# Moving side products of a three-branch recurrent layer by a chunk, and two score products into one PSUM tile

## The chip, the cores and the metric

The kernel runs on one core of a Trainium2 chip. The time is device time in microseconds (us), from start to end of one execution. TensorE (PE) multiplies matrices into PSUM, VectorE (DVE), ScalarE (ACT) and GpSimd (POOL) do the rest, and SyncE (SP) issues most of the loads and stores.

## The reference

Two groups of tokens, a prompt of 256 and 8 sequences of 8 sample tokens, go through two layers of width 2048. One combined input projection feeds three branches, each gated by a SiLU path; three merge gates weigh their projections:

```python
xn = _rmsnorm(x, lp['norm_g'])
proj = (xn @ lp['w_in']).astype(jnp.float32)
u_s5, z_s5, u_lru, z_lru, q, k, v, z_ret, g_s5, g_lru, g_ret = jnp.split(proj, splits, axis=-1)
y_s5, ns_re, ns_im = _s5(u_s5, ...)
y_lru, n_lru, n_conv = _rglru(u_lru, ...)
y_ret, n_ret = _retention(q, k, v, r_ret, pos0, lp['ret_gn_g'])
b_s5 = (y_s5 * jax.nn.silu(z_s5)) @ lp['w_branch_s5']
b_lru = (y_lru * jax.nn.silu(z_lru)) @ lp['w_branch_lru']
b_ret = (y_ret * jax.nn.silu(z_ret)) @ lp['w_branch_ret']
merged = sigmoid(g_s5) * b_s5 + sigmoid(g_lru) * b_lru + sigmoid(g_ret) * b_ret
out = merged @ lp['w_out']
return (x + out), ns_re, ns_im, n_lru, n_conv, n_ret
```

The parts that the change touches are, in `_rglru`, the two block-diagonal gates of the convolved input `xc`

```python
xb = xc.reshape(bsz, s, LRU_BLOCKS, LRU_BLOCK)
r = jax.nn.sigmoid(jnp.einsum('bsnc,ncd->bsnd', xb, w_a).reshape(bsz, s, LRU_WIDTH) + b_a)
i = jax.nn.sigmoid(jnp.einsum('bsnc,ncd->bsnd', xb, w_x).reshape(bsz, s, LRU_WIDTH) + b_x)
```

and in `_retention` (8 heads of 128) the scores and the new state

```python
sc = jnp.einsum('bihd,bjhd->bhij', qc, kc) * dmask[None]
inner = jnp.einsum('bhij,bjhe->bihe', sc, vc)
r_new = r * g_chunk + jnp.einsum('bjhd,bjhe->bhde', kc * zeta[None, :, :, None], vc)
```

## The kernel before

The prompt and sample tokens stand together as 320 columns. The large products run as one main stream on TensorE: the weights come in blocks of 256 output columns, in chunks of 512 input rows (`raw`, 512 KB each, loaded by SP). Each half chunk is split into a high part (`whi`, made by ScalarE, L125) and a low part (`wlo`, made by VectorE, L98) and multiplied three ways into a main PSUM tile `pt`: L1423 (high by high), L1424 (high weight by low input) and L1425 (low weight by high input), 12 matmuls of 320 columns a half chunk, 24 a chunk. Inputs are `xh` and `xl`, or `yhl` for the branch projections of the merge.

Everything else is side work. It is written as Python generators that are advanced once after each half chunk (`step`); a plain `yield` waits two such steps, so a piece behind it is emitted one chunk, 24 main matmuls, later. The order on every engine and queue is the order of emission, fixed when the program is built. Side products take a PSUM tile `ps` of [128, 512] from a pool of four (`ps()`); a fifth must wait until the readers of the first are done.

- `lru_u` convolves the LRU's input on VectorE into `xc` (tile `lxc`), then multiplies it by the gates' weights at L804, one pair of blocks `j` at a time.
- `ret_heads` takes a pair of heads `m`: the prompt's scores of each head go into a tile of their own (L970, L971, columns 0 to 383), the sample scores of both heads into a third (L974), from `kd`, a copy of the sample columns of `k` (tile `rkd`). VectorE reads the sample scores into `scs` and the prompt's scores into `rsc`. Then `k` is transposed (L994) for the state.
- `ret_state` takes the sample states `r0` (in rows, `r`) and adds two products per head (L1108); the result is stored as `ret_s`. Just before, transposes of the pair's output (L1076) go to `z`.
- `merge_blocks` orders the blocks of a merge: gate blocks lead the branch projections by `n` blocks.

The `ret_state` of one pair and the `ret_heads` of the next meet on the engines: four pairs a layer, three such handovers.

Of the kernel before, what the change touches and what calls it, by code (L numbers as in the profile page):

```python
# [20 lines left out]
SEQ, NB, NS, PAST = 256, 8, 8, 2048  # L21
# [57 lines left out]
class Program:  # L79
# [687 lines left out]
    def lru_u(self, l, j, pt):  # L767
        nc, I = self.nc, self.I
        u = self.wt([128, 2, PADW], name="lu")
        self.mul(u[:, :, 3:S0], pt[:, :, :SEQ], self.rs2()[:, :, :SEQ])  # L770
        us = u[:, :, S0:].rearrange("p n (b e) -> p n b e", e=11)
        for n in range(2):
            self.mul(us[:, n, :, 3:], pt[:, n, SEQ:T].rearrange("p (b s) -> p b s", s=NS),
                     self.rstd[:, SEQ:].rearrange("p (b s) -> p b s", s=NS))
        nc.vector.memset(u[:, :, 0:3], 0.0)
        while not self.flag.get(('lru', l)):
            yield
        for n in range(2):
            self.copy(us[:, n, :, 0:3], self.lin[:, 2 * j + n, 0:24].rearrange("p (b k) -> p b k", k=3))
        yield  # L780
        wg = self.wt([128, 2, 2, 128], name="lw")
        nc.sync.dma_start(wg, I['lw'][l, j])
        xc, r, i = [], [], []
        while j and not self.flag.get(('y', l, 0, j - 1)):
            yield
        for n in range(2):
            b = 2 * j + n
            x = self.vt([128, CONVW], name="lxc")
            self.ts(x, u[:, n, 0:CONVW], self.pcol(l, 'convw', b), OP.mult, self.pcol(l, 'convb', b), OP.add)
            for k in range(1, 4):  # L790
                yield 0
                self.stt(x, u[:, n, k:k + CONVW], self.pcol(l, 'convw', 8 * k + b), x, OP.mult, OP.add)
            xc.append(x)
            self.copy(self.lst[:, b, 9:12], u[:, n, SEQ:SEQ + 3])
            self.copy(self.lst[:, b, 12:36].rearrange("p (b k) -> p b k", k=3), us[:, n, :, 8:11])
            yield
        for n in range(2):
            b = 2 * j + n
            r.append(self.vt([128, CONVW + 8], name="lr"))
            i.append(self.vt([128, CONVW], name="li"))  # L800
            pp = []
            for k, dst, key in ((0, r[n][:, :CONVW], 'ba'), (1, i[n], 'bx')):
                p = self.ps()
                nc.tensor.matmul(p[:, :CONVW], wg[:, k, n], xc[n], start=True, stop=True)  # L804
                pp.append((dst, p, key))
            yield
            for dst, p, key in pp:
                self.act(dst, p[:, :CONVW], AF.Sigmoid, bias=self.pcol(l, key, b))
        yield
        while not self.flag.get(('sp', l)):  # L810
            yield
        for n in range(2):
            self.mul(i[n], i[n], xc[n])
            yield 0
        for n in range(2):
            self.act(xc[n], r[n][:, :CONVW], AF.Exp, scale=self.sp8[:, 2 * j + n:2 * j + n + 1])
        yield
        for n in range(2):
            t = r[n][:, :CONVW]
            self.act(t, t, AF.Tanh, scale=self.sp4[:, 2 * j + n:2 * j + n + 1])  # L820
        yield
        for n in range(2):
            self.stt(xc[n], xc[n], 1.0, r[n][:, :CONVW], OP.add, OP.mult)
            yield n
        for n in range(2):
            t = r[n][:, :CONVW]
            self.act(t, t, AF.Sqrt)
            self.ts(xc[n], xc[n], -1.0, OP.mult, 1.0, OP.add)
        yield
        for n in range(2):  # L830
            t = r[n][:, :CONVW]
            self.stt(t, xc[n], 1.0, t, OP.add, OP.mult)
            yield 0
            self.mul(i[n], i[n], t)
            nc.vector.memset(xc[n][:, S0 - 1:S0 + 77:11], 0.0)
            nc.vector.tensor_copy(i[n][:, S0 - 1:S0 + 77:11], self.lin[:, 2 * j + n, 24:32])
            yield 0
            self.dve(xc[n], 2.1)
            nc.vector.tensor_tensor_scan(r[n][:, :CONVW], xc[n], i[n], 0.0, op0=OP.mult, op1=OP.add)
            yield 0  # L840
        while not self.flag.get(('zl', l, j)):
            yield
        z = self.szl.pop(j)
        for n in range(2):
            h = r[n]
            self.copy(self.lst[:, 2 * j + n, 0:1], h[:, SEQ - 1:SEQ])
            self.copy(self.lst[:, 2 * j + n, 1:9], h[:, S0 + 7:S0 + 85:11])
            self.mul(z[:, n, :SEQ], z[:, n, :SEQ], h[:, :SEQ])
            zs = z[:, n, SEQ:].rearrange("p (b s) -> p b s", s=NS)
            self.mul(zs, zs, h[:, S0:S0 + 88].rearrange("p (b e) -> p b e", e=11)[:, :, 0:NS])  # L850
            yield 0
        self.y_parts(l, 0, j, z)
        self.nl += 1
        if self.nl == 4:
            yield
            nc.sync.dma_start(self.O['lru'][l], self.lst)
# [96 lines left out]
    def ret_heads(self, l, m):  # L953
        nc, I, O, sm = self.nc, self.I, self.O, self.sm
# [8 lines left out]
        q, k = self.ret.pop(('q', m)), self.ret.pop(('k', m))  # L963
        kd = self.vt([128, 2, 64], name="rkd")
        self.copy(kd, k[:, :, SEQ:])
        k4 = self.parts_of(k)
        pp, sc = [], []
        for n in range(2):
            p = self.ps()
            nc.tensor.matmul(p[:, :256], k[:, n, 0:128], q[:, n, 0:256], start=True, stop=True)  # L970
            nc.tensor.matmul(p[:, 256:384], k[:, n, 128:256], q[:, n, 128:256], start=True, stop=True)  # L971
            pp.append(p)
        p = self.ps()
        nc.tensor.matmul(p[:, :128], kd.rearrange("p n t -> p (n t)"), q[:, :, SEQ:], start=True, stop=True)  # L974
        yield
        scs = self.scs
        for n in range(2):
# [4 lines left out]
        for n in range(2):  # L982
            t = self.vt([128, 384], name="rsc")
# [6 lines left out]
        for n in range(2):  # L990
            h = 2 * m + n
            p = self.ps()
# [6 lines left out]
        p = self.rows_of(k4)  # L999
# [21 lines left out]
        for n in range(2):  # L1021
            p = self.ps()
# [8 lines left out]
                             start=True, stop=False, skip_group_check=True)  # L1031
            po.append(o)
        for n in range(2):
            o = po[n]
            for h in range(2):
                for g in range(4):
                    nc.tensor.matmul(o[g * 32:(g + 1) * 32, 2], self.qpad[:, n, 2 * g + h], r0[n][:, 2 * g + h],  # L1037
                                     start=False, stop=h == 1, tile_position=(0, g * 32), skip_group_check=True)
# [12 lines left out]
        v, rs, t = (vv[:, i] for i in range(3))  # L1051
# [20 lines left out]
        for n in range(2):  # L1072
            h = 2 * m + n
            p = self.ps()
# [11 lines left out]
    def ret_state(self, l, m, kt, k4, vt, v4, r0):  # L1086


        nc, O, sm = self.nc, self.O, self.sm
        p = self.ps()  # L1090
        for n in range(2):
            for c in range(2):
                nc.tensor.matmul(p[:, n * 128:(n + 1) * 128], kt[:, n, c], vt[:, n, c], start=c == 0, stop=c == 1,  # L1093
                                 skip_group_check=True)
        yield
        rp = self.vt([128, 2, 128], name="rp")
        self.copy(rp.rearrange("p n e -> p (n e)"), p[:, :256])
        yield
        nc.sync.dma_start(O['ret_p'][l][:, 2 * m:2 * m + 2], rp)
        for n in range(2):  # L1100
            h = 2 * m + n
            for b in range(4):
                r = slice(32 * b, 32 * b + 32)
                self.copy(self.vbd[r, :, b], v4[r, n].bitcast(F32))
            yield
            for c in range(2):
                p = self.ps()
                nc.tensor.matmul(p, k4[:, n, c * 128:(c + 1) * 128], self.vbd[:, c].rearrange("p b e -> p (b e)"),  # L1108
                                 start=True, stop=True)
                yield  # L1110
                rr = r0[n][:, 4 * c:4 * c + 4].rearrange("p b e -> p (b e)")
                self.stt(rr, rr, self.g8[h], p, OP.mult, OP.add)
            nc.sync.dma_start(O['ret_s'][l, h], r0[n])
        self.flag['st', l, m] = True
# [145 lines left out]
    def merge_blocks(self, l, br, inp, wb, yb, cg):  # L1260
        def br_blk(j):
            return (wb[j], 8, yb, self.merge, (l, br, j))
        n = 3 if l == 0 and br == 0 else 1
        for j in range(8 + n):
            if j < 8:
                yield inp(cg + 256 * j, self.gate, j)
            if j >= n:
                yield br_blk(j - n)
# [276 lines left out]
```

## Time and profile before

| | us |
|---|---|
| median of 3 runs (2424.43 to 2430.43) | 2425.45 |
| the profiled execution's own time | 2425.49 |
| its span | 2423.7 |
| PE busy | 2369.4 (98%) |
| DVE busy | 1533.1 (63%) |
| ACT busy | 1107.3 (46%) |
| POOL busy | 588.4 (24%) |

The span is the part of the execution that the trace covers. A busy share is a mean over the whole span; what ends a wait is read at each place. [...]

### The profile page before, as it was taken

Reading aid. Unit: us, or ns where it says so; the run is one execution under the profiler, and the core shown is the slowest. Engines: PE = TensorE matmul, PEld = TensorE weight load, DVE = VectorE, ACT = ScalarE, POOL = GpSimd, SP = SyncE. Lnnn points to the kernel's source line nnn. Section 1 sums busy time; section 2 is a strip of 40 time slices with the busy share of each in tenths; the row PEclk is TensorE's granted clock in tenths of the full one; section 3 lists DMA queues with packets and bytes.
Section 4 is the critical chain, followed back from the end, with each engine's and each line's share of the span. In section 5 each row is a group of like instructions: output and inputs, shape, how many; then the busy total and the mean of one; then the engine's idle time right before and its main releaser. Section 6 shows DMA issues by size and latency. Waiting matters only on the chain. (4 is left out here: it accounts for less than half of the span.)

```text
span 2423.7 us, 44413 instructions
## 1 busy us (share of the span) xinstructions
PE 2369.4 (98%) x16778; PEld 2340.4 (97%) x16778; DVE 1533.1 (63%) x2830; ACT 1107.3 (46%) x2019; POOL 588.4 (24%) x1159
## 2 busy tenths in 40 slices
PE   9999999989999999999999999999999999999997
PEld 9999899989999999999999999999999999999997
DVE  7885658656664756755557765866665656555544
ACT  6655444434443534444455564444434434444443
POOL 2020007999211000300100000699930200000011
PEclk9999999999999999999999999999999999999999
DMA  6754775455445545445545587454454554444453
GB/s 229 222 155 144 195 217 168 141 171 171 149 157 174 188 152 172 148 157 196 193 158 187 171 218 209 146 174 151 139 191 162 174 181 160 149 149 150 155 175 130
DMA packets 154023, 413.72 MB, mean 171 GB/s; under 512 B 18640, under 2 KB 60112, under 8 KB 153552
## 3 DMA queue, kind: packets, MB, share of 16 engines
q1 hardware_dynamic: 153232, 410.16, 53.0%
q8 instruction: 132, 2.16, 0.4%
q10 hardware_dynamic: 576, 0.72, 0.1%
q14 instruction: 83, 0.68, 0.1%
HBM read 373.83 MB, written 31.74 MB: 167 GB/s over the span
## 5 line engine op out<-in xcount | busy, mean ns | idle before, releaser
L98 DVE TENSOR_TENSOR wlo<-raw,whi 128x512 fp32r<-128x512 f32 (+1 forms) x1199 | 854.3, 721 | 800.7 <-ACT whi L125 789.8
L125 ACT ACTIVATE whi<-raw 128x512 fp32r<-128x512 f32 (+1 forms) x1199 | 745.8, 629 | 1070.0 <-PE pt L1424 923.0
L1423 PE MATMUL pt<-xh,whi 128*128 128x320 f32 x3352 | 1053.9, 314 | 1.4 <-ACT whi L125 0.9
L1424 PE MATMUL pt<-xl,whi 128*128 128x320 f32 x3352 | 1042.2, 311 | 0.8 <-DVE xl L118 0.8
L1425 PE MATMUL pt<-xh,wlo 128*128 128x320 f32 x3352 | 1042.3, 311 | 0.2 <-DVE wlo L98 0.2
L1423 PEld LDWEIGHTS pt<-xh,whi 128*128 128x128 f32 x3352 | 635.6, 190 | 7.0 <-issue 4.1
L1424 PEld LDWEIGHTS pt<-xl,whi 128*128 128x128 f32 x3352 | 635.4, 190 | 4.8 <-DVE xl L118 1.5
L1425 PEld LDWEIGHTS pt<-xh,wlo 128*128 128x128 f32 x3352 | 634.8, 189 | 0.9 <-DVE wlo L98 0.7
L1423 PE MATMUL pt<-yhl,whi 128*128 128x320 f32 x768 | 239.3, 312 | 2.7 <-ACT yhl L125 2.7
L1425 PE MATMUL pt<-yhl,wlo 128*128 128x320 f32 x768 | 238.0, 310 | 2.9 <-DVE wlo L98 2.9
L1424 PE MATMUL pt<-yhl,whi 128*128 128x320 f32 x768 | 238.1, 310 | 0.2 <-DVE yhl L98 0.2
L598 POOL TENSOR_TENSOR cs<-H,l2r 128x64 f32<-128x64 f32 x254 | 122.5, 482 | 253.2 <-DVE H L112 233.5
L271 POOL TENSOR_TENSOR acc<-acc,sq 128x320 f32<-128x320 f32 x28 | 25.6, 914 | 591.7 <-ACT sq L125 590.6
L1423 PE MATMUL pt<-M,whi 128*128 128x320 f32 x512 | 158.4, 309 | 0.0
L1425 PE MATMUL pt<-M,wlo 128*128 128x320 f32 x512 | 158.2, 309 | 0.0
L1424 PE MATMUL pt<-M,whi 128*128 128x320 f32 x512 | 158.2, 309 | 0.0
L1423 PEld LDWEIGHTS pt<-yhl,whi 128*128 128x128 f32 x768 | 144.8, 188 | 3.6 <-ACT yhl L125 2.9
L1425 PEld LDWEIGHTS pt<-yhl,wlo 128*128 128x128 f32 x768 | 144.7, 188 | 3.1 <-DVE wlo L98 3.1
L1424 PEld LDWEIGHTS pt<-yhl,whi 128*128 128x128 f32 x768 | 144.8, 188 | 0.6 <-DVE yhl L98 0.6
L601 POOL TENSOR_TENSOR H<-cs,cs 128x64 f32<-128x64 f32 x254 | 121.1, 477 | 19.9
L599 POOL TENSOR_TENSOR cs<-H,l2i 128x64 f32<-128x64 f32 x254 | 119.9, 472 | 0.0
L600 POOL TENSOR_TENSOR cs<-cs,H 128x64 f32<-128x64 f32 x254 | 118.1, 465 | 0.0
(255 smaller groups left out, 2445.2 us busy)
## 6 DMA issues: line engine op xcount, KB each, us to landing
raw<-w_in SPq DMA_DIRECT2D x447, 512.0 KB, 4.2
raw<-w_out SPq DMA_DIRECT2D x64, 512.0 KB, 4.1
raw<-wb_lru SPq DMA_DIRECT2D x32, 512.0 KB, 4.1
raw<-wb_ret SPq DMA_DIRECT2D x32, 512.0 KB, 3.8
raw<-wb_s SPq DMA_DIRECT2D x32, 512.0 KB, 3.6
r<-sret SPq DMA_DIRECT2D x16, 512.0 KB, 5.2
ret_s<-r SPq DMA_DIRECT2D x16, 512.0 KB, 3.0
raw<-w_glu SPq DMA_DIRECT2D x16, 512.0 KB, 3.6
```

The source lines that it names most:

```text
L98: self.nc.vector.tensor_tensor(o, a, b, op=op)
L125: self.nc.scalar.activation(o, a, f, **k)
L271: self.nc.gpsimd.tensor_tensor(self.acc, self.acc, sq, op=OP.add)
L598: g.tensor_tensor(t1, old, lr, op=OP.mult)
L599: g.tensor_tensor(t2, self.swap(old), li, op=OP.mult)
L600: g.tensor_tensor(t1, t1, new, op=OP.add)
L601: g.tensor_tensor(new, t1, t2, op=OP.add)
L1423: nc.tensor.matmul(o, hi[:, kk, cs], xh, start=k == 0, stop=False)
L1424: nc.tensor.matmul(o, hi[:, kk, cs], xl, start=False, stop=False)
L1425: nc.tensor.matmul(o, lo[:, kk, cs], xh, start=False, stop=k == nk - 1)
```

## The change

Five edits. The gate products of `lru_u` stand one more `yield` behind the last write of `xc`. In `ret_heads` a `yield` stands between the copy `kd` and the scores, and the sample scores go into columns 384 to 511 of the first head's tile rather than into a tile of their own. In `ret_state` a second `yield` stands ahead of the products of each head. In the first merge of layer 0 four gate blocks lead, where three did.

```diff
@@ -794,6 +794,7 @@
             self.copy(self.lst[:, b, 12:36].rearrange("p (b k) -> p b k", k=3), us[:, n, :, 8:11])
             yield
+        yield
         for n in range(2):
             b = 2 * j + n
@@ -963,6 +964,7 @@
         kd = self.vt([128, 2, 64], name="rkd")
         self.copy(kd, k[:, :, SEQ:])
+        yield
         k4 = self.parts_of(k)
@@ -970,8 +972,8 @@
             pp.append(p)
-        p = self.ps()
-        nc.tensor.matmul(p[:, :128], kd.rearrange("p n t -> p (n t)"), q[:, :, SEQ:], start=True, stop=True)
+        p = pp[0][:, 384:]
+        nc.tensor.matmul(p, kd.rearrange("p n t -> p (n t)"), q[:, :, SEQ:], start=True, stop=True)
         yield
@@ -1102,6 +1104,7 @@
                 self.copy(self.vbd[r, :, b], v4[r, n].bitcast(F32))
             yield
+            yield
             for c in range(2):
@@ -1260,7 +1263,7 @@
-        n = 3 if l == 0 and br == 0 else 1
+        n = 4 if l == 0 and br == 0 else 1
```

Line numbers of the changed kernel are one to three higher: L804 becomes L805, L970 and L971 become L972 and L973, L974 becomes L976, L994 becomes L996, L1076 becomes L1078, L1108 becomes L1111 and L1423 becomes L1426.

TensorE at the first handover of layer 0, before. `ps_6535` takes transposes that `z` will read, `ps_6544` and `ps_6547` the next pair's scores, `ps_6550` the sample scores, `ps_6571` the last state product; the rows left out are main matmuls.

```order
L1076 MATMUL ps_6535<-ident_603,ron_6333 128x128 x3
L970 MATMUL ps_6544<-ra_6199,ra_6378 128x256 [waits DVE_49]
L971 MATMUL ps_6544<-ra_6199,ra_6378 128x128
L970 MATMUL ps_6547<-ra_6199,ra_6378 128x256 [waits PE_49]
L971 MATMUL ps_6547<-ra_6199,ra_6378 128x128
L974 MATMUL ps_6550<-ra_6199,rkd_6539 128x128 [waits DVE_49,Activation_49]
L1423 MATMUL pt_6518<-xh_164,whi_6479 128x320
...
L1108 MATMUL ps_6571<-vbd_5306,rk4_5975 128x512 [waits DVE_49,PE_49]
```

The same place in the changed kernel. `ps_6579` and `ps_6582` take the scores, `ps_6604` and `ps_6655` the last two state products.

```order
L1078 MATMUL ps_6532<-ident_603,ron_6332 128x128 x3
...
L972 MATMUL ps_6579<-ra_6198,ra_6377 128x256 [waits DVE_49]
L973 MATMUL ps_6579<-ra_6198,ra_6377 128x128
L972 MATMUL ps_6582<-ra_6198,ra_6377 128x256 [waits PE_49]
L973 MATMUL ps_6582<-ra_6198,ra_6377 128x128
L976 MATMUL ps_6579<-ra_6198,rkd_6536 128x128 [waits Activation_49]
L1426 MATMUL pt_6515<-xh_270,whi_6516 128x320
...
L1111 MATMUL ps_6604<-vbd_5306,rk4_6016 128x512
...
L1111 MATMUL ps_6655<-vbd_5306,rk4_6016 128x512 [waits DVE_49,PE_49]
...
L996 MATMUL ps_6677<-ident_603,ra_6377 128x128 [waits DVE_49,PE_49]
```

The scores stand 24 main matmuls behind the transposes instead of right behind them, both last state products stand behind the scores, 24 main matmuls apart, and the next pair's transposes follow 12 behind the last of them. The sample scores wait for ScalarE alone; the transposes wait for VectorE, which they did not at this place before.

ScalarE in the first merge, before. `yhl_3120` is the input of the branch projection's fourth input block, made from `z_1987`; `g_3057` is a gate.

```order
L125 ACTIVATE g_3057<-g_3057 128x640 [waits DVE_49]
L125 ACTIVATE H_2777<-ps_3013 64x2x168 x2
L125 ACTIVATE whi_3084<-raw_2963 128x512 [waits PE_49,Activation_49]
...
L125 ACTIVATE yhl_3120<-z_1987 128x640 [waits DVE_49]
```

The same in the changed kernel, where it is `yhl_3286`, and `g_3283` is the fourth gate.

```order
L125 ACTIVATE whi_3267<-raw_3174 128x512 [waits DMAHW4_49,PE_49,Activation_49]
L125 ACT_TABLE_LOAD [waits DMAHW6_49,DMAHW5_49,DMAHW7_49,DMAHW1_49]
L125 ACTIVATE g_3283<-g_3283 128x640 [waits DVE_49]
L125 ACTIVATE yhl_3286<-z_1977 128x640
```

The copy into `yhl` stands behind the fourth gate's sigmoid and a table load. On TensorE the products that use it follow the fourth gate's block by 36 main matmuls.

## Rows read from the trace of the kernel before

**Rows 1.** The page, busy time of TensorE (us, share of the span, instructions).

```profile
PE 2369.4 (98%) x16778; PEld 2340.4 (97%) x16778; DVE 1533.1 (63%) x2830; ACT 1107.3 (46%) x2019; POOL 588.4 (24%) x1159
```

**Rows 2.** TensorE's waits over the span: us in total, times, longest.

```profile
PE ps L974 <- DVE r L118: 13.7, 6, 3.9
PE ps L1108 <- DVE z L118: 6.7, 4, 2.2
PE ps L1108 <- DVE scs L98: 3.8, 2, 1.9
...
PE pt L1423 <- ACT yhl L125: 2.7, 1, 2.7
PE ps L804 <- DVE k L98: 2.4, 1, 2.4
PE ps L581 <- issue: 1.7, 1, 1.7
PE ps L804 <- DVE lxc L118: 1.5, 1, 1.5
...
PE ps L970 <- DVE ra L98: 0.9, 2, 0.5
```

**Rows 3.** Busy time of the engines by stretch; PEclk is TensorE's granted clock.

```profile
225.00:232.00 7.00, 5.88 (x24) 4.95 (x25) 0.81 (x3) 2.89 (x7) 0.53 (x2) 0.76 0.04 12
262.00:272.50 10.50, 7.32 (x30) 6.85 (x31) 5.60 (x14) 4.16 (x13) 0.00 (x0) 0.67 0.77 200
493.00:508.00 15.00, 8.76 (x42) 7.78 (x41) 4.98 (x9) 2.55 (x6) 13.59 (x37) 0.77 0.30 106
573.00:583.00 10.00, 7.39 (x30) 7.16 (x31) 4.45 (x11) 1.78 (x4) 9.06 (x26) 0.66 0.20 76
645.00:655.00 10.00, 7.30 (x30) 7.07 (x31) 3.85 (x10) 1.88 (x4) 0.00 (x0) 0.66 0.15 62
986.00:998.00 12.00, 8.62 (x57) 8.09 (x56) 10.64 (x10) 3.45 (x6) 11.84 (x9) 1.00 0.34 112
1689.00:1703.00 14.00, 8.11 (x42) 7.44 (x43) 4.33 (x9) 2.98 (x7) 12.59 (x36) 0.88 0.27 101
1768.00:1778.00 10.00, 7.76 (x32) 7.53 (x33) 3.88 (x10) 2.14 (x5) 9.06 (x26) 0.66 0.13 54
1840.00:1846.00 6.00, 4.44 (x19) 4.21 (x20) 1.68 (x4) 1.25 (x3) 0.00 (x0) 0.72 0.23 89
```

The columns are us, then busy us (and instructions) of PE, PEld, DVE, ACT and POOL, then PEclk, the DMA share and GB/s.

**Rows 4.** TensorE's timeline at the first handover of layer 0: start, us, instruction, wait.

```profile
499.17 0.46 PE L974 MATMUL ps<-ra,rkd 128*128 128x128 f32 x2 [3.91 <-DVE r L118]
...
499.91 0.31 PE L1423 MATMUL pt<-xh,whi 128*128 128x320 f32 x1
500.05 0.31 PE L1424 MATMUL pt<-xl,whi 128*128 128x320 f32 x1
...
501.16 0.47 PE L1423 MATMUL pt<-xh,whi 128*128 128x320 f32 x1
501.42 0.47 PE L1424 MATMUL pt<-xl,whi 128*128 128x320 f32 x1
...
504.07 0.77 PE L1108 MATMUL ps<-vbd,rk 128*128 128x512 f32 x1 [1.92 <-DVE scs L98]
```

**Rows 5.** ScalarE's and VectorE's timelines just ahead of that L974.

```profile
496.16 0.63 ACT L125 ACTIVATE whi<-raw 128x512 fp32r<-128x512 f32 x1 [1.58 <-DMA raw<-w_in]
498.35 0.67 DVE L118 SCALAR_TENSOR_TENSOR r<-r,ps 128x512 f32<-128x512 f32 x1
```

**Rows 6.** ScalarE's and VectorE's timelines in the first merge, up to the late `yhl`.

```profile
256.86 1.28 ACT L125 ACT_TABLE_LOAD   x1
260.34 0.74 ACT L125 ACTIVATE g<-g 128x640 f32<-128x640 f32 x1 [2.20 <-DVE g L98]
...
264.81 0.74 ACT L125 ACTIVATE yhl<-z 128x640 fp32r<-128x640 f32 x1 [1.39 <-DVE z L98]
...
265.58 0.83 DVE L98 TENSOR_TENSOR yhl<-z,yhl 128x640 fp32r<-128x640 f32 x1 [0.80 <-ACT yhl L125]
```

## The prediction

> **What bounds the kernel now.** I began with the page's busy time per engine: TensorE (PE) is busy 2369.4 of 2423.7 us [rows 1], so only its idle time and the clock at which it runs can give much. Next I read its waits, longest first [rows 2]. Three places in the program hold most of them. In retention, the sample scores L974 wait six times for a VectorE `r` update (13.7 us) and the state products L1108 six times for `z` or `scs` (6.7 + 3.8), with 0.9 before L970: 25.1 us. In the LRU of layer 0, the gate products L804 wait 2.4 and 1.5. In the first merge, S5's L581 waits 1.7 and the first product of `yhl` 2.7. Six and six over two layers is one wait of each sort at every handover from one head pair to the next (four pairs a layer, three handovers).
>
> Third, the granted clock around these places [rows 3]. [...] The window at 986 to 998 holds a wait too, and PE busy only 8.62 of 12 us, yet stays at 1.00. [...]
>
> Fourth, why L974 waits. It needs its own PSUM tile, the third of the pair beside two score tiles; four side tiles turn round, and the next free one holds a state product of the pair before, which VectorE adds into `r`. That addition stands behind a weight's low half in VectorE's queue, whose high half waited 1.58 us for its load; the addition runs at 498.35 for 0.67 us and L974 starts at 499.17 [rows 4, 5]. So a late weight reaches TensorE through a buffer, ahead of the time at which the weight itself would be missed.
>
> **The change, part by part.** *Shared tile, kd yield, state yield (retention).* Instructions are only moved, none is added. By the first pair of order listings, L974 now writes the tile whose other columns the first head's scores have just taken, and its wait for VectorE is gone; what it waits for, ScalarE's copy `kd`, is emitted a chunk (24 main matmuls, 24 x 0.147 = 3.5 us, the spacing from rows 4) ahead. The scores too stand a chunk later, behind `ra`, which was 0.4 us late. The third state product has no wait left. The fourth still waits for `z`, but stands 60 main matmuls behind the transposes that `z` reads, where it stood 12 behind them: 8.8 us instead of 1.8, against waits of at most 2.2. So I take all 25.1 us as gone. Lower bound: the 11.4 us of L1108 and L970 stay, since the new places have waits of their own; upper bound 25.1.
>
> With the waits I let the low clock go. Of the 34 us, the 1.92 us wait at 504.07 lies inside its stretch [rows 4]; of the five other waits for `z` and `scs` (8.6 us by rows 2) I take about 3 as inside. That leaves 29 us of work, x 0.45 = 13. Bounds: 10.6 if all of the waits lie inside, 15.3 if none does; 0 if the clock falls all the same. Retention: 25.1 + 13 = 38.1.
>
> What is late next? The transposes of the next pair (L994; L996 in the listing) now wait for VectorE's read of the shared tile, a wait that this place did not have. Behind it on TensorE stands the whole main stream. From the fourth state product to there TensorE has half a chunk, and from the sample scores two chunks, 7 us; in these VectorE must do two low halves, a `yhl` and four products of scores, some 0.2 to 0.9 us each: about 4. I cost it at nothing, with 2 to 3 us of cover; uncovered, the nearest row is a wait for `z`, 6.7/4 = 1.7 us each. [...]
>
> The stores of `ret_s` are moved a place or so back in SP's queue, since the last addition comes later; the loads that stood behind them now stand ahead. That can only bring the weight of rows 5 sooner. A load behind the second store is later, and needed two chunks on; I cost it at nothing, and if its cover went it would show as a 1.58 us wait like that of rows 5.
>
> *LRU yield.* L804 stands a chunk, 3.5 us, further behind its operand, against waits of 2.4 and 1.5 [rows 2]: gone, with 3.4 x 0.45 = 1.5 of clock. Later steps of the LRU move along, and in layer 1, where no such wait is among the rows, they have room. Gain 2.4 + 1.5 + 1.5 = 5.4 (bounds 0 and 5.4).
>
> *Four gates ahead.* The product of `yhl` for block 3 comes 96 main matmuls later, 14 us; the LRU chain that makes it comes 72 later, 10.6 us, since its products, too, stand behind. That should leave 3.5 us against a 2.7 us wait. But in the second pair of listings ScalarE makes `yhl` only after a gate's sigmoid, and that gate's block ends just 36 main matmuls (5.3 us) ahead of the need. Within these lie a buffer's release (12 matmuls, 1.8), a high half (0.63 as in rows 5), a low half and the gate's product (about 0.8 each, as `yhl` on VectorE), the sigmoid and the `yhl` copy (0.74 each) [rows 6], then 0.83 on VectorE a matmul later: 6.3 against 5.4. I keep a 1.0 us wait (bounds 0 and 2.7) and let L581's 1.7 go. The clock held at 1.00 through the longer wait of the untouched window [rows 3], so I let this low stretch go: 6.9 less 0.8 of idle, x 0.45 = 2.7. Gain 2.7 + 1.7 + 2.7 - 1.0 = 6.1 (bounds 0 and 7.3). ScalarE gets two more table loads, 1.28 us each; the one of before lay in 2.20 us of idle ahead of a sigmoid [rows 6], and I cost them at nothing.
>
> **Sum.** 38.1 + 5.4 + 6.1 = 49.6. The profiled execution's own time is 2425.49 us, practically the median of 2425.45, so 2425.5 - 49.6 = 2376 us.
>
> **Rivals.**
> - *The new wait bites.* L994 waits at six handovers, 1.7 us each and with a short low stretch of 3.4 x 0.45 = 1.5: 6 x 3.2 = 19, so 2395; without the clock 2386. For it: one tile now serves four readers, and VectorE is the engine that was late. Against: the 2 to 3 us of cover above.
> - *The merge stays as it is.* `yhl` and L581 wait as before and the clock falls: 6.1 less gained, 2382. For it: `yhl` is emitted just where it is needed. Against: the 3.5 us.
> - *The clock falls all the same.* Idle time goes, the low stretches stay: 13 + 1.5 + 2.7 = 17 us, so 2393. Against: each of the eight low windows holds one of the removed waits. [...]
> - *It doesn't do what it says.* The late weight is the true cause, and TensorE stands at the weight instead of at the buffer: 2425. Against: the weight of rows 5 is used by matmuls that, in the program's order, stand a chunk or more behind L974.
> - *Slower.* The shared tile holds each of the eight head pairs (not six handovers only) as long as the longest wait of rows 4, 3.9 us, with a full low stretch, 6.9 x 0.45 = 3.1: 8 x 7.0 = 56, so 2432. It decides from 49.6/8 = 6.2 us per pair, over twice the length of any wait of rows 2 but the 3.9.
>
> **How the numbers follow.** A measurement of this kernel tells about 0.3% (7 us) from no change. Chances: forecast 0.62 (its own range 2370 to 2381, from the bounds of clock and merge), merge as before 0.15, new wait 0.10, clock 0.06, no effect 0.03, slower 0.04. The range 2370 to 2392 holds the first two, the new wait without the clock and some of the rest, about 0.85. Faster 0.93; same 0.03; slower 0.04.
>
> **What would show it.** No wait of L974 (L976 by the new numbers) for `r`, none of the state products, and windows of the handovers at clock 1.00; no wait of the LRU gate products in layer 0; one wait of about 1 us at `yhl` before the first merge's fourth block. I am wrong if the transposes behind the scores wait for `rsc`, if first products of a weight wait for `whi` at the handovers, or if low clock shows without a wait.

## The result, and the profile after

The changed kernel takes 2372.76 us (median of 4 runs, 2372.36 to 2372.87), the kernel before 2425.77 beside it: a ratio of 0.9778 (95% interval 0.9761 to 0.9795), 53.0 us less. The forecast was 2376, its range 2370 to 2392.

The page of the changed kernel, busy time by engine, beside [rows 1]:

```profile
PE 2349.4 (99%) x16778; PEld 2324.5 (98%) x16778; DVE 1537.7 (65%) x2830; ACT 1107.6 (47%) x2021; POOL 606.3 (26%) x1159
```

The same 16778 matmuls are busy for 20.0 us less. The span fell by 52.6 us (2423.7 to 2371.1), so 32.6 are idle time. Most of the 20.0 is the clock, by the estimate below, but not all. In the kernel before, the six stretches of retention at a granted clock of 0.50 (a share of full speed), the first and their sum, and in the changed kernel the sample scores at the first handover (two products, which took 0.46 us behind their wait in [rows 4]):

```profile
500.32:507.15 6.83, 4.91 (x19) 4.44 (x18) 1.40 (x4) 0.63 (x1) 6.12 (x19) 0.50 0.01 2
...
sum 34.14, PE 29.34 PEld 28.21 DVE 8.04 ACT 2.96 POOL 21.39; mean PE 4.89 PEld 4.70 DVE 1.34 ACT 0.49 POOL 3.57
```

```profile
485.62 0.39 PE L976 MATMUL ps<-ra,rkd 128*128 128x128 f32 x2
```

TensorE is busy for 29.34 us in these six, and with 3.4 and 5.8 in those of the LRU (227.26 to 230.67) and the merge (264.80 to 271.63), at 0.50 too, for 38.6. At the start of the first, beside [rows 4]:

```profile
499.61 0.31 PE L1424 MATMUL pt<-xl,whi 128*128 128x320 f32 x1
...
500.20 0.36 PE L1425 MATMUL pt<-xh,wlo 128*128 128x320 f32 x1
500.36 0.47 PE L1423 MATMUL pt<-xh,whi 128*128 128x320 f32 x1
...
501.69 0.47 PE L1425 MATMUL pt<-xh,wlo 128*128 128x320 f32 x1
```

Main matmuls start 0.59/4 = 0.147 us apart at 1.00 and 1.33/5 = 0.266 at 0.50, so about 0.45 of each microsecond is lost there. By this estimate the eight stretches cost 17.3 us; one new stretch at 0.50, 3.4 us from 956.57 on, takes 1.5 back. So the clock gave 15.8, and 4.2 us of busy time are something else. Another estimate, which no run isolates: a main matmul of 0.31 us starts 0.147 us behind the one before it [rows 4], so at a wait the last one stands uncovered for 0.16 us, and the first behind it takes some 0.07 longer (the scores' 0.46 against 0.39); with 10 waits in the list where there were 28, that makes 4.1. TensorE's waits of the changed kernel, beside [rows 2]:

```profile
PE pt L1428 <- DVE wlo L98: 3.1, 2, 2.9
...
PE pt L1426 <- ACT yhl L125: 0.7, 1, 0.7
PE ps L1185 <- ACT sq L125: 0.5, 1, 0.5
PE pt L1427 <- DVE yhl L98: 0.4, 1, 0.4
PE ps L581 <- DMA ust<-dul: 0.2, 1, 0.2
```

No L976, no L1111, no L805 is left among them. One line of the program, the sample scores L976 (L974 before), with what its engine waited for:

```profile
L976 PE MATMUL ps<-ra,rkd x16: 275/275/275, 420.8 to 1790.6; 128*128 128x128 f32 x16
its engine sat idle before it (us, times) until:
who waited for it (us, times):
```

All 16 run at the same 275 ns, and the lists of waits are empty. Busy time by stretch, for the LRU, the first merge, the first handover of layer 0 and the place where S5's setup of layer 1 runs, beside [rows 3] (us; then PE, PEld, DVE, ACT and POOL busy, granted clock, DMA share, GB/s):

```profile
228.00:236.00 8.00, 8.00 (x49) 7.21 (x48) 3.85 (x8) 3.10 (x7) 0.00 (x0) 1.00 0.96 241
268.00:278.50 10.50, 9.36 (x77) 8.66 (x76) 7.85 (x16) 7.11 (x14) 0.00 (x0) 1.00 0.36 93
484.00:500.00 16.00, 16.00 (x112) 15.77 (x111) 11.80 (x24) 7.17 (x16) 14.67 (x34) 1.00 0.63 193
950.00:966.00 16.00, 13.09 (x79) 12.83 (x78) 14.61 (x15) 4.21 (x8) 15.37 (x12) 0.89 0.32 102
```

The handover is busy throughout at a granted 1.00, where it had 8.76 of 15 us at 0.77, and the other five are too, 16.00 of 16 us each at 1.00. The last row is the one of these with a low clock, 0.89, and a wait that was there before; the runs come back to it. The first merge keeps a wait; ScalarE's timeline there:

```profile
267.41 1.28 ACT L125 ACT_TABLE_LOAD   x1
269.55 0.74 ACT L125 ACTIVATE g<-g 128x640 f32<-128x640 f32 x1 [0.85 <-DVE g L98]
270.19 0.72 ACT L125 ACTIVATE yhl<-z 128x640 fp32r<-128x640 f32 x1
```

The table load lies in idle time ahead of the gate, and `yhl` follows the sigmoid at once: the order of emission is what makes it late, not its operand. (With one gate more ahead the wait goes; that run stands below.)

### The profile page after: what moved, and what is told of

Read it like the earlier page. It is cut to its first block, busy times and chain, and to the rows that moved or that the text cites. A ratio compares the mean times of both kernels' runs of the same rounds, so it can differ in the third digit from the quotient of the medians.

```text
span 2371.1 us, 44404 instructions
## 1 busy us (share of the span) xinstructions
PE 2349.4 (99%) x16778; PEld 2324.5 (98%) x16778; DVE 1537.7 (65%) x2830; ACT 1107.6 (47%) x2021; POOL 606.3 (26%) x1159
## 4 chain that ended last, share of the span: by engine, by line
PE 98%; DVE 1%; DMA 1%; ACT 0%; issue 0%; SPq 0%; ACTq 0%; DVEq 0%
PE pt L1426 31%; PE pt L1427 30%; PE pt L1428 30%; PE ps L678 1%; PE ps L805 1%; PE ps L581 1%; PE ps L1039 0%; PE ps L1111 0%; PE ps L1095 0%; PE ps L951 0%; PE ps L972 0%; DMA raw<-wb_lru 0%; PE ps L1078 0%; DMA xin<-x 0%; PE ps L670 0%
## 5 line engine op out<-in xcount | busy, mean ns | idle before, releaser
L1426 PE MATMUL pt<-xh,whi 128*128 128x320 f32 x3352 | 1049.3, 313 | 1.2 <-ACT whi L125 1.1
L1426 PEld LDWEIGHTS pt<-xh,whi 128*128 128x128 f32 x3352 | 629.6, 188 | 7.2 <-issue 3.5
L1426 PE MATMUL pt<-yhl,whi 128*128 128x320 f32 x768 | 238.9, 311 | 0.7 <-ACT yhl L125 0.7
L598 POOL TENSOR_TENSOR cs<-H,l2r 128x64 f32<-128x64 f32 x254 | 133.0, 524 | 240.4 <-DVE H L112 220.7
L1426 PE MATMUL pt<-M,whi 128*128 128x320 f32 x512 | 158.4, 309 | 0.0
L1426 PEld LDWEIGHTS pt<-yhl,whi 128*128 128x128 f32 x768 | 144.8, 189 | 1.1 <-ACT yhl L125 1.0
L599 POOL TENSOR_TENSOR cs<-H,l2i 128x64 f32<-128x64 f32 x254 | 127.8, 503 | 0.0
L601 POOL TENSOR_TENSOR H<-cs,cs 128x64 f32<-128x64 f32 x254 | 114.7, 452 | 19.9
```

The costliest lines, as they stand in the source:

```text
L598: g.tensor_tensor(t1, old, lr, op=OP.mult)
L599: g.tensor_tensor(t2, self.swap(old), li, op=OP.mult)
L601: g.tensor_tensor(new, t1, t2, op=OP.add)
L1426: nc.tensor.matmul(o, hi[:, kk, cs], xh, start=k == 0, stop=False)
```

## The experiments

Three theories stood beside each other for retention, where most of the gain lies. A, that of the prediction: what counts is how much is emitted between the reader that frees a side tile and the product that takes it. B: the third tile alone is the cause. C: the yields alone do it. The kernel before ran at 2425.8 to 2427.7 us on the chips used, so each kernel is set against the kernel before on its own chip.

**One edit alone: the shared tile.** The kernel before with

```diff
-        p = self.ps()
-        nc.tensor.matmul(p[:, :128], kd.rearrange("p n t -> p (n t)"), q[:, :, SEQ:], start=True, stop=True)
+        p = pp[0][:, 384:]
+        nc.tensor.matmul(p, kd.rearrange("p n t -> p (n t)"), q[:, :, SEQ:], start=True, stop=True)
```

> The kernel before with one edit: the sample scores share the first head's tile. Theory A (tile release: what counts is how much emission lies between the reader that frees a side tile and the product that takes it, so tile and both yields are needed together): L974 no longer waits for r, but the fourth state product takes the tile that the r addition frees and waits for r instead, at the first handover about 2 us in place of 3.9, at the others about 1.3; retention's idle time falls from 25 to some 10 us and part of the low clock stays: 2396 to 2412, I say 2403. Theory B (the third tile alone is the cause, the yields in retention add nothing): retention's whole gain of about 38 us comes with it: 2388. Theory C (the yields alone do it, the tile nothing): 2425.

Measured: 2399.06 beside 2427.68, ratio 0.9881 (0.9866 to 0.9895), 28.6 us less. Its waits in retention:

```profile
PE ps L1108 <- DVE r L118: 9.5, 6, 2.4
...
PE ps L970 <- DVE ra L98: 0.7, 2, 0.3
```

The wait for `r` went from L974 to the state product, as A says, and retention's 25.1 us became 10.2. B's 2388 is out, C's 2425 too. By estimate about 1.5 of the 28.6 us (3.4 x 0.45) do not belong to the edit: the LRU's low stretch, whose waits are unchanged, is missing in this trace, at 1.00 over 225 to 232 (last section).

**The changed kernel less one edit of retention, three times.** The sample scores back in a tile of their own; the `yield` before the state products out; the one behind `kd` out:

```diff
-        p = pp[0][:, 384:]
-        nc.tensor.matmul(p, kd.rearrange("p n t -> p (n t)"), q[:, :, SEQ:], start=True, stop=True)
+        p = self.ps()
+        nc.tensor.matmul(p[:, :128], kd.rearrange("p n t -> p (n t)"), q[:, :, SEQ:], start=True, stop=True)
```

> The changed kernel with the sample scores back in a tile of their own, all yields and four gates kept. Theory A: L976's own tile is freed a chunk ahead, so it hardly waits, but the fifth tile makes the state product behind it take the tile that z frees, 12 main matmuls after z is emitted: waits of 0.5 to 2 us at six handovers, with some low clock: 2380 to 2395, I say 2384. Theory B: the r wait is back at L976, 2405 to 2411. Theory C: no difference, 2373.

```diff
                 self.copy(self.vbd[r, :, b], v4[r, n].bitcast(F32))
             yield
-            yield
```

> The changed kernel without the second yield before the state products. Theory A: the last state product stands ahead of the next pair's scores again, and the scores take the tile that the r addition or z frees with half a chunk between: waits at L972 of 1 to 2 us at six handovers, with some low clock: 2380 to 2395, I say 2386. Theories B and C apart: B expects 2373, C 2390 or more.

```diff
         self.copy(kd, k[:, :, SEQ:])
-        yield
```

> The changed kernel without the yield between kd and the scores. Theory A: scores stand right behind the transposes again; L970's wait for ra (0.4 us at two handovers) and a wait for kd of at most 0.4 come back; the state products stay a chunk or more behind and wait for nothing; 2373 to 2379, I say 2375. Theory B: 2373. Theory C: this yield carries a good part, 2385 or more.

Measured, all beside 2427.68: 2374.60 (ratio 0.9780, 0.9765 to 0.9794), 2376.88 (0.9791, 0.9777 to 0.9806) and 2377.34 (0.9790, 0.9774 to 0.9806). The changed kernel's own ratio is 0.9778, so none of the three costs more than about 3 us when it is taken away, with intervals of 3.4 to 3.9 us either way. One wait row of each that the changed kernel doesn't have, in the same order:

```profile
PE ps L1111 <- DVE scs L98: 2.1, 2, 1.7
```

```profile
PE ps L972 <- DVE r L118: 4.5, 2, 2.8
```

```profile
PE ps L971 <- DVE ra L98: 3.7, 6, 1.5
```

In each case a wait appears at the product that A named, but not as A had it: in the first two at two handovers rather than six, and in the first for `scs`, not for `z`; in the third at six rather than two, up to 1.5 us rather than 0.4. A's times for the first two (2380 to 2395) were missed, and with them its claim that the tile and both yields are needed together; only the third lies in its range. C holds as far as this: beside both yields the shared tile is worth nothing that these runs can tell. Its 2390 and 2385 or more for the other two are out, since one yield and the tile do as well. One yield without the tile was not tried. The three edits overlap; any two of them do nearly all of it, and the tile by itself two thirds.

**Retention alone.** The kernel before with the three edits of retention; LRU and merge untouched.

> The kernel before with the three edits of retention alone. If the parts add up (theory A): 2425.8 less the retention's share, so that what is left above the changed kernel is the LRU's waits with their low clock (1.5 + 2.4 + 0.4 + 1.5 = 5.8) and the merge's (1.7 + 2.9 + 2.7 less the 1.1 that stays = 6.2): ratio 2384.8/2425.8 = 0.983, 2383 to 2387. Rival: the clock is shared between places (fewer pauses earlier give a full clock later), so the LRU and merge lose less: 2380 or less.

Measured: 2384.79 beside 2426.89, ratio 0.9828 (0.9811 to 0.9844), 42.1 us less. That is as expected (2383 to 2387), and the rival's 2380 or less is out. The LRU's and the merge's waits are those of [rows 2]. One of the waits of this trace is new:

```profile
PE ps L995 <- DVE rsc L98: 0.6, 1, 0.6
```

It is the rival's wait of the transposes (L994 before) for the readers of the shared tile, once instead of six times.

**Three gates, and no yield in the LRU.** The changed kernel with `n = 3` again, and the changed kernel without the first of its yields:

```diff
-        n = 4 if l == 0 and br == 0 else 1
+        n = 3 if l == 0 and br == 0 else 1
```

> The changed kernel with three gates ahead, LRU yield kept. Theory A: the yhl chain still comes 72 main matmuls (10.6 us) later while its use goes back 96: the wait for yhl grows to 8 to 10 us, with a low clock of up to 3 us: 2372.8 + 11 = 2384, 2380 to 2387, ratio 0.983. Rival: the fourth gate does nothing, since yhl is made in slack anyway: 2375 or less.

```diff
             yield
-        yield
         for n in range(2):
             b = 2 * j + n
             r.append(self.vt([128, CONVW + 8], name="lr"))
```

> The changed kernel without the LRU yield, four gates kept. Theory A: the gate products of layer 0 wait again for lxc and k (1.5 + 2.4 + 0.4, perhaps 1.5 of clock), while yhl comes up to 72 main matmuls earlier and its 1.1 us wait is gone: 2376 to 2378, ratio 0.980. Rival: with a block more ahead the LRU chain has slack and the waits cost nothing: 2372.

Measured, beside 2426.89: 2383.15 (ratio 0.9823, 0.9809 to 0.9838) and 2375.44 (0.9791, 0.9777 to 0.9806). The wait at `yhl` of the first, then the LRU's waits of the second:

```profile
PE pt L1426 <- ACT yhl L125: 9.4, 1, 9.4
```

```profile
PE ps L804 <- DVE k L98: 2.4, 1, 2.4
...
PE ps L804 <- DVE lxc L118: 1.5, 1, 1.5
```

The waits came as A forecast, and the first time; the second lies 0.6 us below its range of 2376 to 2378. With three gates the LRU yield mostly moves the wait to `yhl`, which grows from 2.7 to 9.4 us: set against retention alone (2384.79) that yield brings 1.6 us by itself, four gates 9.4 by themselves, and both together 12. Part of the 9.4 can be clock: the whole trace of retention alone was granted 0.995, that of the kernel without the LRU yield 0.997.

**The late store.** This one tries the chain behind L974's wait in the kernel before: a store of `ret_s` waits for `r` in SP's queue, the weight behind it comes late, with it VectorE's low half and the addition behind that. SP's wait at the first handover of the kernel before:

```profile
SPq L1113 <- DVE r L118: 2.0, 1, 2.0
```

The stores move behind the last state product:

```diff
-            nc.sync.dma_start(O['ret_s'][l, h], r0[n])
         self.flag['st', l, m] = True
+        yield
+        for n in range(2):
+            nc.sync.dma_start(O['ret_s'][l, 2 * m + n], r0[n])
```

> The kernel before, with the two stores of the new sample states moved behind the last state product and one chunk further, so that they no longer stand in SP's queue ahead of weights while they wait for r. If the chain late store, late weight, late r addition, late L974 holds: the weight at the first handover lands about 2 us earlier and L974's 3.9 us wait falls to 1.5 to 2 at the two first handovers, the others (1.3 to 1.8, with another cause, z) change little: 2425.8 - 4 to 8 = 2418 to 2422. Rival: the store is not what holds the weight, 2425.8.

Measured: 2416.36 beside 2426.89, ratio 0.9959 (0.9944 to 0.9975), 10.5 us less. First a row of ScalarE's timeline, then one of VectorE's, the counterparts of [rows 5]:

```profile
492.56 0.62 ACT L125 ACTIVATE whi<-raw 128x512 fp32r<-128x512 f32 x1
...
494.68 0.67 DVE L118 SCALAR_TENSOR_TENSOR r<-r,ps 128x512 f32<-128x512 f32 x1
```

and TensorE's waits:

```profile
PE ps L974 <- DVE r L118: 11.7, 6, 2.2
PE ps L1108 <- DVE scs L98: 4.1, 2, 2.1
PE ps L1108 <- DVE z L118: 3.1, 4, 0.9
```

The high half no longer waits for its load, the addition runs 3.7 us sooner (the scores L970 ahead of it 1.9 us), and the longest wait falls from 3.9 to 2.2: the chain holds for the first handovers of the layers. But six waits of 1.7 to 2.2 stay. At three of the four other handovers L974 even waits longer, 1.7 to 2.1 us where it was 1.3 to 1.4, and the `z` waits right behind are shorter; that was not forecast. The gain is above the 4 to 8 us expected, about 1.5 of it, by estimate, the LRU's low stretch, which is missing in this trace too (1.00 over 225 to 232). So the store made the longest wait longer; that the scores take a tile right behind the product that it comes from makes the wait at all, as the two kernels without it show (the shared tile alone, and both yields with the tile apart).

**What the changed kernel still waits for.** At 955.8 it waits 2.9 us for a low half `wlo`, with the 0.89 of the 950 to 966 row. VectorE's timeline of the changed kernel there (a row that counts several gives their time together):

```profile
953.06 1.10 DVE L118 SCALAR_TENSOR_TENSOR l2i<-lamr,lami 128x32 f32<-128x32 f32 x1
954.19 0.97 DVE L112 TENSOR_SCALAR l2i<-l2i 128x32 f32<-128x32 f32 x1
955.08 3.86 DVE L98 TENSOR_TENSOR wlo<-raw,whi 128x512 fp32r<-128x512 f32 x3
958.86 0.81 DVE L98 TENSOR_TENSOR g<-pt,rstd 128x640 f32<-128x640 f32 x1
```

A low half takes 3.86/3 = 1.29 us here, and 0.69 in the median of the whole trace; GpSimd is busy 15.37 of 16 us. Four kernels on one chip: the changed kernel with the five products of `l2r` and `l2i` moved ahead of those that let GpSimd start; with five gates ahead; with both; and unchanged.

```diff
-        self.ts(nr, lamr, -1.0, OP.add)
         den, t2, cre, cim = col(), col(), col(), col()
-        self.mul(den, lr0, lr0)
...
-        yield 0
         l2r = self.pl.tile([128, 32], F32, name="l2r", tag="l2r")
...
         self.l2r, self.l2i = l2r, l2i
+        yield 0
+        self.ts(nr, lamr, -1.0, OP.add)
+        self.mul(den, lr0, lr0)
...
```

> The changed kernel with the five small VectorE products of l2r and l2i in S5's setup moved ahead of those that start GpSimd's chain. In the trace of the changed kernel they take 0.97 to 1.24 us each while GpSimd is busy (0.18 to 0.2 when it is not), and the low half wlo behind them comes 2.9 us late at 955.8, with 3.4 us at the lower clock. Theory D (these five products are what makes wlo late): about 4 us of VectorE time goes from the stretch, wait and low clock go: 2372.8 - 4.4 = 2368.4, 2368 to 2370. Rival E (GpSimd slows the low halves themselves, 1.29 instead of 0.69 us each, and these alone make them late): about half of it stays, 2371 to 2373.

```diff
-        n = 4 if l == 0 and br == 0 else 1
+        n = 5 if l == 0 and br == 0 else 1
```

> The changed kernel with five gates ahead in the first merge. If the 0.7 + 0.45 us wait for yhl is only its emission in the slot where it is needed, a block more removes it: 2371.6 beside 2372.8. Rival: the tenth work buffer or SP's queue of S5 weights stands still for the fifth gate, 2374 or more.

> Both of these together: they lie 680 us apart and should add up, 2367.2 by theory D, 2370 to 2372 by E.

> The changed kernel itself on the same chip as the three others, to set them against: 2372.8 if this chip runs the kernel before at 2425.8, else in proportion.

Measured: 2369.28 (2368.79 to 2370.27), 2370.54 (2370.24 to 2371.43), 2368.19 (2367.32 to 2368.70) and 2372.39 (2371.96 to 2372.58). In the first, VectorE's timeline has these rows:

```profile
944.94 0.19 DVE L118 SCALAR_TENSOR_TENSOR l2i<-lamr,lami 128x32 f32<-128x32 f32 x1
945.16 0.18 DVE L112 TENSOR_SCALAR l2i<-l2i 128x32 f32<-128x32 f32 x1
...
950.75 3.87 DVE L98 TENSOR_TENSOR wlo<-raw,whi 128x512 fp32r<-128x512 f32 x3
...
956.68 6.51 DVE L98 TENSOR_TENSOR wlo<-raw,whi 128x512 fp32r<-128x512 f32 x4 [1.33 <-ACT whi L125]
```

and of its waits for a low half this is left:

```profile
PE pt L1428 <- DVE wlo L98: 0.8, 1, 0.8
```

The moved products take 0.18 to 0.19 us, where four of the five took 0.97 to 1.24; the low halves stay at 1.29. The wait at 955.8 is gone, and its low stretch, it seems, with it: the whole trace was granted 0.998, that of the changed kernel as run beside it 0.997. What is left, 0.8 us, stands at a later low half, at 958.6, beside four that take 6.51/4 = 1.63 us each. So D's products were most of it, and E's slower low halves are likely the 0.8; that was not tried by itself, and GpSimd's chain also starts about 2 us later than in the changed kernel. The gain is 3.1 us of D's 4.4: in the changed kernel as run beside these the wait is 1.9 us, not 2.9, with the same 0.89 over 950 to 966.

Five gates give 1.9, more than the 1.2 expected, and both together 4.2, less than their sum; 2367.2 was expected of both. The `yhl` wait of 1.1 is gone. The rest can be clock: with five gates alone the low half still waits, 2.8 us, but at 1.00 (last section), so the low stretch that the moved products would remove is already missing there. The kernel with both is the fastest, at 0.9759 of the kernel before (0.9745 to 0.9772).

## Why the prediction was right, step by step

The mechanism was right and so was the time, to 3.2 us. Of the 49.6 us forecast 32.4 were idle time and 17.2 clock; the trace gives 32.6 of idle time and, by the estimate above, 15.8 of clock and 4.2 that the sum did not have. The prediction has no row beside its 34, 6.9 and 3.4 us of low clock and its 0.45; the trace of the kernel before shows 34.14, 6.83 and 3.41 us at a granted 0.50, and the 0.45 follows from the starts of the main matmuls, 0.147 us apart at 1.00 and 0.266 at 0.50.

*Retention* was priced at 38.1 and gave 42.1 alone (37.9 to 45.9 by its interval, so the runs cannot tell the two apart). All 25.1 us of waits went, as forecast. The clock's term, "x 0.45 = 13", was right too: it took 29 us of work in the six low stretches, and TensorE is busy there for 29.34. What is missing is a term for busy time beyond the clock, the 4.2 us of the result's section. That the sum came so close is in part luck: this term and the new low stretch, 1.5 us the other way, partly cancel.

*What is late next* was right in the changed kernel: the transposes don't wait there, and the trace of retention alone, with one wait of 0.6, says how thin the cover is. The shared tile took 28.6 us away by itself and changed nothing measurable beside the yields, and that one wait is the only cost of it that a trace shows.

*LRU and merge* were priced at 5.4 and 6.1, 11.5 together, and gave 12 together. The division between them was wrong in kind: the LRU yield brings 1.6 alone and four gates 9.4 alone, since whatever delays the LRU's products delays `yhl` with them. (The bound of 7.3 for the merge is 7.1 by its own terms.) The 1.0 us kept at `yhl` came as 0.7 + 0.4, in the order that the listing showed.

*The untouched window* was taken as proof that its wait leaves the clock at 1.00. In the changed kernel the same wait has 0.89 over 16 us, 3.4 of them at 0.50, so the argument does not hold. The merge's 2.7 us of clock rested on it. That stretch did go to 1.00 (268 to 278.5), but for a reason that no run shows.

## What to carry to other kernels

Where side work takes tiles from a small pool, read each wait of a product as two distances in emission order: from the last reader of the tile to its next taker, and from an operand to its use. One step more of either, or one tile fewer taken per group, can end the same wait, so several such edits overlap and their gains must not be added; a step added early in a chain (the LRU) brings little until the use at its end (the merge) moves back too: 1.6 us alone, about 3 beside four gates. Around the waits look for stretches at a lower granted clock, too: here eight at 0.50 cost 17 us by estimate (38.6 busy us x 0.45), beside 33 us of idle time. Price them by the busy time inside them.

## What the runs showed of the hardware

In these traces the lower clock does not follow from the length of a wait. The LRU's wait of 2.4 us at 226 is the same in the kernel before, with the shared tile alone, and with retention alone; the rows of the latter two for this stretch, the shared tile first:

```profile
225.00:232.00 7.00, 5.77 (x34) 5.05 (x35) 1.74 (x5) 4.08 (x9) 0.54 (x2) 1.00 0.04 12
```

```profile
225.00:232.00 7.00, 5.42 (x21) 4.43 (x22) 1.01 (x3) 2.51 (x7) 0.53 (x2) 0.76 0.04 12
```

1.00 in one and 0.76, as in [rows 3], in the other. The wait for a low half that no edit of the change touches behaves alike: 2.8 us with five gates, 1.9 in the changed kernel as run beside it, and their rows, in this order:

```profile
947.00:963.00 16.00, 12.64 (x84) 12.10 (x83) 14.54 (x19) 4.72 (x8) 14.21 (x12) 1.00 0.36 118
```

```profile
950.00:966.00 16.00, 14.04 (x84) 13.51 (x83) 14.54 (x18) 4.49 (x9) 14.96 (x11) 0.89 0.34 103
```

The longer wait kept 1.00. What decides it was not tried and stays open. One execution of each kernel was traced, so it may differ between executions of one kernel too. By estimate, a difference of some 1.5 us between two kernels (3.4 us x 0.45) can therefore be such a stretch at a place that neither edit touches.

In the trace of the changed kernel some of VectorE's work was slower beside GpSimd's products of 1.1 to 1.7 us, and some was not: a low half, with both inputs in SBUF, took 1.29 us instead of 0.69, the product of `l2i` with one input 0.97 instead of the 0.18 that it took when moved ahead, and the gate's product from PSUM 0.81, as it does elsewhere (0.82 in the median of 48). What divides them was not tried. How busy GpSimd is does not decide alone: in the handover at 484 to 500 it is busy 14.67 of 16 us, with products of 0.33 to 0.93 us, and low halves take 0.68 to 0.81 there.
